# Input combinations by transposes and shared passes, first weights split a product ahead, bias tables read from one reversed row, log1p as a series

## The chip, the cores and the metric

One core of a Trainium2 chip runs the whole program. It has five engines with instruction queues of their own: TensorE (PE, matrix products; PEld is its loading of weights), VectorE (DVE), ScalarE (ACT), GpSimd (POOL) and SyncE (SP), and 16 DMA engines that move data between HBM and the core's memories SBUF and PSUM. DMAs are issued from a queue of an engine, here nearly all from SP and some from POOL and ACT. The metric is the device time of one execution in microseconds, as the median of several.

## The reference

One layer of an encoder runs on two inputs with shared weights: a sequence of 1024 rows ("A") and one of 512 rows ("B"), each row 1024 wide. Cut to what matters:

```python
h = rms_norm(x, pre_w)
cols = h @ w_in                     # q|k, v, o, z, gates of the mLSTM; q, k, v, z of the attention; merge gates
qk = silu(centred_dwconv(m_qk))     # short convolution along the rows
li = m_i + i_bias;  lf = log_sigmoid(m_f + f_bias)
y_m = mlstm(q, k, v, li, lf, both directions) * sigmoid(o) * silu(z)
# attention: 3 dilation groups x 8 heads x 64, each with a band of keys
logits = q @ k.T + bias_table[bucket(key - query)]
y_a = denominator_weighted_mix(softmax parts of the 3 groups) * silu(a_z)
merged = sig(g_A) * (y_m @ w_pm) + sig(g_B) * (y_a @ w_pa)
y = x + rms_norm(merged @ w_out, post_w)
```

Everything is float32. The products are made from a high and a low part of each operand (hi = rounded copy, lo = rest): three passes of PE, hi*hi, hi*lo and lo*hi (mm3, L206 to L211).

## The kernel before, in words

The 1024 rows of A and the 1024 columns of D are each cut in two halves of 512, so the input is a 2x2 matrix of blocks (a0, b0 for the first 512 rows, a1, b1 for the others). The input projection of A multiplies these with 2x2 blocks of weights by a scheme of seven block products in place of eight, which needs sums of the input's blocks (the seven names B11, T2, B21, T3, T1, T4, B22) and sums of the weights' blocks. Each of the seven combinations of the input is kept turned (features on partitions, rows along the free side) as a hi part H[0] and a lo part H[1] of four chunks of 128x512.

combos (L371 to L441) makes them, in group 0 of the values. lead and norm scale the rows; sub forms differences of blocks on DVE in place. put(m, k) makes one chunk of combination m in one PSUM bank. For T1 and T2 it turns four 128x128 blocks by transposes (L428). For B21 and B22 it turns them by float32 matmuls with the identity as the moving operand (L430). T3 and T4 have two terms: the first is turned by a transpose, the second added by a float32 matmul with plus or minus the identity (L430 again). A float32 matmul or a transpose of 128x128 shows as two records each or as one. Then ACT copies the bank to the hi part (L432); the lo part is DVE's difference (L434), or for B21 and B22 a pass of PE that subtracts the hi part in the bank (L438, with minus the identity as weights) and a second ACT copy (L439). The names in the profile: x is a block, d a PSUM bank, Hh and Hl the hi and lo parts, minus lies in a part of Hl.

value_group (L454 to L662) makes one of four groups of 322 value columns: products m1 (of B11), m2 (B21), m6 (T2), m7 (T3), m5 (T1), m4 (T4), m3 (B22), each of 48 passes of 128x322 in four banks. Weights arrive as va and vb (two halves of 644 KB each; SP issues them, L466 and L468, and each has one buffer); sums (L444 to L449) makes their sums with three DVE operations of 128x1288; split (L472 to L480) makes hi on ACT and lo on DVE. In group 0 the puts of the combinations are put between the passes of the products m1, m2, m7 and m6: with_m1 makes B21, with_m2 makes B22 and the first chunks of T3, and so on. u2 and u3 are running sums in SBUF; out writes a result part out by ACT (L509), DVE (L510) and an SP store (L511). The scheduler keeps each engine's program in the order in which the code issues the work, except that split runs with high priority, and issue_after pins an instruction behind another.

Then the unit pairs follow (unit_pair, L704): for each pair of 128 columns the same seven products of 128x512, weights loaded by SP (pw_raw, L682), summed on POOL (psum_w) and split by ACT and DVE (phla and phlb, L668 and L669). After the pairs the results are convolved or activated, and stored by SP (aqk_a, L219).

bias_tables (L342) makes, on 32 rows, for each of four cases of dilation and eight heads the bias by offset: a row of 512 numbers (erow, 2 KB in HBM). bias_copies (L360) copies two rows 128 times each to erep (512 KB), called once after a pair for 16 pairs, on SP behind that pair's weight loads. In the attention, table (L1322) loads for two heads the band of 128 partitions by a diagonal read of erep (a step of 511 from partition to partition), and DVE adds it to the logits (L1374).

lanes (L929) makes the logarithms of the gates on 64x128 tiles: log_sigmoid(x) = min(x, 0) - log1p(exp(-|x|)). log1p is made from Ln and Exp on ACT, with a correction, in L948 to L954. Such functions need another function table, whose loading shows as ACT_TABLE_LOAD. For B the generator lanes is advanced at chosen steps of the attention of A.

Of the kernel before, what the change touches and what calls it, by code (L numbers as in the profile page):

```python
# [29 lines left out]
P = 128  # L30
# [10 lines left out]
EL = 512  # L41
OW = 132
# [139 lines left out]
class Net:  # L182
# [23 lines left out]
    def mm3(self, out, lhs, rhs, start, stop):  # L206
        nc = self.nc
        (lh, ll), (rh, rl) = lhs, rhs
        nc.tensor.matmul(out, lh, rh, start=start, stop=False)  # L209
        nc.tensor.matmul(out, lh, rl, start=False, stop=False)  # L210
        nc.tensor.matmul(out, ll, rh, start=False, stop=stop)  # L211
# [127 lines left out]
    def bias_tables(self, sb, ps, dram):  # L339
# [18 lines left out]
        self.erep = dram.tile([m, 8, P, EL], F32, name="erep")  # L358

    def bias_copies(self, j, after):  # L360

        i, h = divmod(2 * j, 8)
        with self.tc.issue_after(after.ins):
            self.nc.sync.dma_start(self.erep[i, h:h + 2],
                                   self.erow[8 * i + h:8 * i + h + 2][:, None, :].to_broadcast([2, P, EL]))
# [6 lines left out]
    def combos(self, ps, H, xt, r, junk, pw, minus, again, diag):  # L372
# [45 lines left out]

        def put(m, k):
# [3 lines left out]
            p = ps.tile([P, BLK], F32, name="d")  # L423
            for t in range(4):
                for i, (x, one) in enumerate(terms[m]):
                    of, to = x[t][:, k * P:(k + 1) * P], p[:, t * P:(t + 1) * P]
                    if i == 0 and m not in (B21, B22):
                        nc.tensor.transpose(to, of, one)  # L428
                    else:
                        nc.tensor.matmul(to, of, one, start=t == i == 0, stop=True, skip_group_check=True)  # L430
# [13 lines left out]
    def sums(self, wa, wb, s):  # L444
# [4 lines left out]
        nc.vector.tensor_sub(s[:, 1], s[:, 0], wa[:, 0])  # L449
# [4 lines left out]
    def value_group(self, g, T, H, sb, us, co, ps, late=None, begin=None, u3=None, more=None, turn=None):  # L454
# [8 lines left out]
        if g:  # L463
            first, wa, wb, s = place(), *self.value_weights(sb)
            for kh in range(2):
                nc.sync.dma_start(wa[:, kh], self.a["w_vp"][g, 0, kh])  # L466
            for kh in range(2):
                nc.sync.dma_start(wb[:, kh], self.a["w_vp"][g, 1, kh])  # L468
        else:
            first, wa, wb, s, (lead, norm, sub, put) = begin  # L470

# [10 lines left out]
        def product(m, w, turns=(), outer=False):  # L482

            banks = [ps.tile([P, BLK], F32, name="d") for _ in range(4)]
# [3 lines left out]
            for i in range(4):  # L488
                for j in range(4):
# [3 lines left out]
                             k == 0, k == 3)  # L493
# [27 lines left out]
        if g == 0:  # L521
# [44 lines left out]
            def with_m7():  # L566
# [6 lines left out]
                put(T2, 0), put(T2, 1)  # L573
                yield
                put(T2, 2), put(T2, 3)
# [24 lines left out]
            with self.tc.issue_after(low[1]):  # L600
                s2 = split(s[:, 1])
# [8 lines left out]
        else:  # L610
            self.sums(wa, wb, s)
# [1446 lines left out]
```

## Time and profile before

| | |
|---|---|
| median of 3 runs | 2242.16 us (2238.9 to 2243.58) |
| the profiled execution, its own time | 2237.88 us |
| its span | 2236.1 us |
| PE busy | 2222.0 us, 99% of the span, clock granted 1.0 throughout |
| DVE, ACT, POOL busy | 1517.3, 1125.7 and 706.6 us |

The profiled execution's time is 1.8 us longer than its span, the part around the first and the last instruction. A row of a group gives busy time and the mean of one instruction; since matmuls overlap in PE's pipeline, the time from the start of one to the start of the next is what one costs, not its own duration. In the timeline the brackets at the end of a row tell how long the engine stood idle ahead of it, and what ended that.

### The profile page before, as it was taken

To read this page: it belongs to the slowest core of one execution; us is meant where nothing else is said; L and a number is where in the kernel's file an instruction comes from. 1 tells how busy PE (TensorE), PEld (TensorE's weight loads), DVE (VectorE), ACT (ScalarE), POOL (GpSimd) and SP (SyncE) were. 2 spreads that over 40 slices of the span, in tenths; PEclk is the share of its full clock that TensorE was granted. 3 is DMA by queue.
4 is the path that set the end of the run, shared out by engine and by line. 5 is a ranking of instruction groups with operands and counts; after the bars stand their busy time and mean duration, and the time that the engine had idled before them with its cause. 6 is when DMAs were issued, how large, how long until landed. Compare 5 with 4: busy or idle time off the path is not lost.

```text
span 2236.1 us, 35149 instructions
## 1 busy us (share of the span) xinstructions
PE 2222.0 (99%) x12050; PEld 1945.2 (87%) x12050; DVE 1517.3 (68%) x2975; ACT 1125.7 (50%) x2397; POOL 706.6 (32%) x976
## 2 busy tenths in 40 slices
PE   9999999999999999999999999999999999999998
PEld 8999878888888888888888889999888888888887
DVE  7765577677777655548887765565689855655774
ACT  6332244444444343447776665666665644554332
POOL 1000333343333222236677620011165522221221
PEclk9999999999999999999999999999999999999999
DMA  3552445543333222375755769997678888776663
GB/s 124 154 150 74 175 180 211 197 172 126 109 109 113 85 85 91 124 273 195 233 168 181 202 176 248 258 262 230 203 242 293 253 263 233 236 261 195 238 229 110
DMA packets 221788, 417.21 MB, mean 187 GB/s; under 512 B 24969, under 2 KB 128073, under 8 KB 221610
## 3 DMA queue, kind: packets, MB, share of 16 engines
q1 hardware_dynamic: 193640, 314.81, 44.2%
q0 software_dynamic: 24368, 87.56, 12.6%
q10 hardware_dynamic: 3602, 12.59, 1.4%
q8 instruction: 96, 1.57, 0.3%
q14 instruction: 82, 0.67, 0.1%
HBM read 295.14 MB, written 128.12 MB: 189 GB/s over the span
## 4 chain that ended last, share of the span: by engine, by line
PE 93%; DMA 3%; DVE 1%; issue 1%; ACT 1%; POOL 0%; DVEq 0%; POOLq 0%; SPq 0%; ACTq 0%
PE d L211 13%; PE d L210 13%; PE d L209 13%; PE dense L209 12%; PE dense L211 12%; PE dense L210 12%; PE o L1406 3%; PE pt L1385 2%; PE lg L1360 2%; PE num L209 1%; PE num L211 1%; PE num L210 1%; DMA vs_a<-vz 1%; PE a L1076 1%; PE kv L209 1%
## 5 line engine op out<-in xcount | busy, mean ns | idle before, releaser
L209 PE MATMUL dense<-H,wh 128*128 128x512 f32 x664 | 270.2, 407 | 0.0
L211 PE MATMUL dense<-H,wl 128*128 128x512 f32 x664 | 260.6, 393 | 0.0
L210 PE MATMUL dense<-H,wh 128*128 128x512 f32 x664 | 260.5, 392 | 0.0
L211 PE MATMUL d<-Hh,phla 128*128 128x512 f32 x608 | 236.8, 389 | 0.5 <-DVE phla L669 0.5
L209 PE MATMUL d<-Hh,phla 128*128 128x512 f32 x608 | 236.6, 389 | 0.5 <-ACT phla L668 0.5
L210 PE MATMUL d<-Hl,phla 128*128 128x512 f32 x608 | 236.5, 389 | 0.0
L278 DVE TENSOR_TENSOR wl<-wraw,wh 128x1024 fp32r<-128x1024 f32 (+1 forms) x121 | 149.2, 1234 | 66.0 <-ACT wh L272 65.7
L1374 DVE CUSTOM_DVE_ANT_0 ls<-lg,bias 128x256 f32<-128x256 f32 (+2 forms) x336 | 103.1, 333 | 117.8 <-PE lg L1360 53.5
L211 PE MATMUL d<-Hh,phlb 128*128 128x512 f32 x456 | 177.4, 389 | 0.0
L209 PE MATMUL d<-Hh,phlb 128*128 128x512 f32 x456 | 177.4, 389 | 0.0
L210 PE MATMUL d<-Hl,phlb 128*128 128x512 f32 x456 | 177.4, 389 | 0.0
L687 POOL TENSOR_TENSOR psum_w<-pw_raw 128x512 f32<-128x512 f32 x38 | 59.5, 1565 | 367.1 <-DMA pw_raw<-w_in 205.6
L1378 ACT ACTIVATE ls<-ls,nm 128x128 f32<-128x128 f32 (+1 forms) x288 | 125.3, 437 | 93.8 <-DVE nm L1376 61.4
L272 ACT ACTIVATE wh<-wraw 128x1024 fp32r<-128x1024 f32 (+1 forms) x124 | 128.7, 1038 | 70.7 <-PE dense L210 27.1
L211 PEld LDWEIGHTS dense<-H,wl 128*128 128x128 f32 x664 | 124.7, 188 | 27.9
L209 PE MATMUL d<-vhi,Hh 128*128 128x322 f32 x448 | 140.9, 314 | 0.3
L211 PE MATMUL d<-vhi,Hl 128*128 128x322 f32 x448 | 140.2, 313 | 0.4 <-DVE Hl L396 0.2
L210 PE MATMUL d<-vlo,Hh 128*128 128x322 f32 x448 | 139.7, 312 | 0.1
L210 PEld LDWEIGHTS dense<-H,wh 128*128 128x128 f32 x664 | 125.3, 189 | 14.3
L209 PEld LDWEIGHTS dense<-H,wh 128*128 128x128 f32 x664 | 125.1, 188 | 14.5
L211 PEld LDWEIGHTS d<-Hh,phla 128*128 128x128 f32 x608 | 114.1, 188 | 24.8 <-DVE phla L669 1.2
L209 PEld LDWEIGHTS d<-Hh,phla 128*128 128x128 f32 x608 | 114.1, 188 | 24.5 <-ACT phla L668 1.0
(572 smaller groups left out, 6116.3 us busy)
## 6 DMA issues: line engine op xcount, KB each, us to landing
pw_raw<-w_in SPq DMA_DIRECT2D x76, 512.0 KB
wraw<-w_in SPq DMA_DIRECT2D x64, 512.0 KB
aqk_a<-pwk SPq DMA_DIRECT2D x48, 512.0 KB
aqk_b<-sw SPq DMA_DIRECT2D x48, 256.0 KB
wraw<-w_pm POOLq DMA_DIRECT2D x24, 512.0 KB, 6.1
wraw<-w_out POOLq DMA_DIRECT2D x24, 512.0 KB, 3.9
wraw<-w_v POOLq DMA_DIRECT2D x22, 430.0 KB, 6.8
erep<-erow SPq DMA_DIRECT2D x16, 512.0 KB
```

The lines of the kernel that those rows point to most:

```text
L209: nc.tensor.matmul(out, lh, rh, start=start, stop=False)
L210: nc.tensor.matmul(out, lh, rl, start=False, stop=False)
L211: nc.tensor.matmul(out, ll, rh, start=False, stop=stop)
L272: high = nc.scalar.activation(hi[:, :n], raw[:, :n], AF.Copy)
L278: low = (self.lows or nc.vector).tensor_sub(lo[:, :n], raw[:, :n], hi[:, :n].bitcast(F32))
L687: self.nc.gpsimd.tensor_add(s[:, 0], ws[1][:, 0], ws[1][:, 1])
L1076: nc.tensor.matmul(p[:, c - c0], kT[:, ct, c * P:(c + 1) * P], qT[:, ct, c * P:(c + 1) * P], start=ct == 0, stop=ct == 1)
L1360: nc.tensor.matmul(lg[:, hh], q[hh][:, qs], z.rearrange("p (n j) -> p n j", j=P)[:, pair], start=z is k[hh], stop=z is not k[hh])
L1374: nc.vector.tensor_tensor_reduce(out=ls[rows, hh], in0=ts["lg"][hh][rows, of], in1=bt[rows, hh, by], scale=1.0, scalar=NEG, op0=OP.add, op ...
L1378: self.held = self.held[-3:] + [nc.scalar.activation(ls[:, hh], ls[:, hh], AF.Exp, bias=nm[:, hh:hh + 1], accum_out=ot[:, 128 + hh:129 + hh])]
L1385: nc.tensor.transpose(pp[:, hh * nk + x], ts["ls"][:, hh, x * P:(x + 1) * P], self.ident)
L1406: nc.tensor.matmul(po[:, hh * 64:hh * 64 + 64], pt[:, hh * nk + x], vh(kt[x], hh), start=x == 0, stop=x == nk - 1)
```

## The change

- put turns B21, B22 and T3's first term by transposes only. T3 is now a1 turned minus the split B22, made by two 128x512 passes (hi and lo part of B22, minus the identity as weights); its sign is turned, so u3 = u2 - m7 here and in the unit pairs. T4 is made from the split B21 and T2 by four such passes, without a transpose, with a plus identity made by one ACT copy. B22 takes over the bank of B21. One put of T2 moves a chunk earlier.
- In group 0, m2 is added on the banks of m1 by PE, and the sum is copied out by ACT instead of added by DVE. The last sum of weights moves behind the start of m7, the split for m7 and the difference T1 move ahead of m2.
- For groups 1 to 3 the loads of va and vb are issued by POOL and the first split of the next group is placed behind m4 (opening); the split for m3 stands ahead of that, the sums behind the split; out of m4 stands behind the split.
- The bias rows are stored reversed; erep and its 16 copies go; table reads erow itself, one element further per partition, and DVE reads the table backwards.
- log1p is a series on DVE in e/(2+e) (with a reciprocal), without Ln and the second Exp on ACT. For B lanes has one more stop, and is advanced at every 8th step instead of every 10th.

```diff
 EL = 512
+LOG1P = [1.0 / ((2 * k + 1) * 4 ** k) for k in range(1, 9)]
...
-    return m.reshape(-1, EL)
+    return m.reshape(-1, EL)[:, ::-1]
...
-        self.erep = dram.tile([m, 8, P, EL], F32, name="erep")
-
-    def bias_copies(self, j, after):
-
-        i, h = divmod(2 * j, 8)
-        with self.tc.issue_after(after.ins):
-            self.nc.sync.dma_start(self.erep[i, h:h + 2],
-                                   self.erow[8 * i + h:8 * i + h + 2][:, None, :].to_broadcast([2, P, EL]))
...
-        plus, neg = self.ident, minus.bitcast(F32)
-        terms = {B21: [(b0, plus)], B22: [(b1, plus)], T3: [(b1, plus), (a1, neg)],
-                 T1: [(a0, plus)], T2: [(b1, plus)], T4: [(b0, plus), (b1, neg)]}
+        turned = {B21: b0, B22: b1, T3: a1, T1: a0, T2: b1}
+        others = {T3: [(B22, minus)], T4: [(B21, plus), (T2, minus)]}
         def lead():
             ps_ = [ps.tile([P, BLK], F32, name="d") for _ in range(4)]
...
                 else:
                     nc.vector.tensor_sub(b1[t], b1[t], a0[t])
+        banks = {}
+
         def put(m, k):
             if m == T4 and k == 0:
                 again()
-            p = ps.tile([P, BLK], F32, name="d")
-            for t in range(4):
-                for i, (x, one) in enumerate(terms[m]):
-                    of, to = x[t][:, k * P:(k + 1) * P], p[:, t * P:(t + 1) * P]
-                    if i == 0 and m not in (B21, B22):
-                        nc.tensor.transpose(to, of, one)
-                    else:
-                        nc.tensor.matmul(to, of, one, start=t == i == 0, stop=True, skip_group_check=True)
+            p = banks.pop((B21, k)) if m == B22 else ps.tile([P, BLK], F32, name="d")
+            banks[m, k] = p
+            begun = m in turned
+            for t in range(4) if begun else ():
+                nc.tensor.matmul(p[:, t * P:(t + 1) * P], turned[m][t][:, k * P:(k + 1) * P], self.ident, is_transpose=True,
+                                 start=t == 0, stop=True, skip_group_check=True)
+            for of, one in others.get(m, ()):
+                for x in range(2):
+                    nc.tensor.matmul(p, one, H[x][of][:, k], start=not begun, stop=True, skip_group_check=True)
+                    begun = True
             hi, lo = H[0][m][:, k], H[1][m][:, k]
             nc.scalar.activation(hi, p, AF.Copy)
             if m not in (B21, B22):
...
-        nc.vector.tensor_sub(s[:, 1], s[:, 0], wa[:, 0])
+        return lambda: nc.vector.tensor_sub(s[:, 1], s[:, 0], wa[:, 0])
...
-        if g:
-            first, wa, wb, s = place(), *self.value_weights(sb)
-            for kh in range(2):
-                nc.sync.dma_start(wa[:, kh], self.a["w_vp"][g, 0, kh])
-            for kh in range(2):
-                nc.sync.dma_start(wb[:, kh], self.a["w_vp"][g, 1, kh])
-        else:
-            first, wa, wb, s, (lead, norm, sub, put) = begin
-
...
+        def opening(g):
+            wa, wb = (sb.tile([P, 2, N], F32, name=x, bufs=1) for x in ("va", "vb"))
+            for j, w in enumerate((wa, wb)):
+                for kh in range(2):
+                    nc.gpsimd.dma_start(w[:, kh], self.a["w_vp"][g, j, kh])
+            return wa, wb, split(wa[:, 0]), self.splits[1]
+
+        if g:
+            wa, wb, w11, early = self.opened
+            s = sb.tile([P, 2, N], F32, name="vsum", bufs=1)
+        else:
+            first, wa, wb, s, (lead, norm, sub, put) = begin
+
+        def product(m, w, turns=(), outer=False, onto=None):
+
+            banks = onto or [ps.tile([P, BLK], F32, name="d") for _ in range(4)]
             turns = iter(turns)
             if outer:
                 next(turns)
...
                     self.mm3(banks[t][:, :VW], (H[0][m][:, k, ts], H[1][m][:, k, ts]), (w[0][:, k], w[1][:, k]),
-                             k == 0, k == 3)
+                             k == 0 and onto is None, k == 3, skip_group_check=onto is not None)
...
-                put(T2, 0), put(T2, 1)
+                put(T2, 0), put(T2, 1), put(T2, 2)
                 yield
-                put(T2, 2), put(T2, 3)
+                put(T2, 3)
...
-                self.sums(wa, wb, s)
-            m2 = product(B21, w12, with_m2())
+                last = self.sums(wa, wb, s)
+            w7 = split(wb[:, 0])
+            with self.tc.issue_after(low[0]):
+                sub(T1)
+            m2 = product(B21, w12, with_m2(), onto=m1)
             held = []
             for t in range(4):
                 held.append(tile_("u2b", 4))
-                add(held[t], u2[t], m2[t][:, :VW])
-            with self.tc.issue_after(low[0]):
-                sub(T1)
-            m7 = product(T3, split(wb[:, 0]), with_m7())
+                nc.scalar.activation(held[t], m2[t][:, :VW], AF.Copy)
+            m7 = product(T3, w7, with_m7())
+            with self.tc.issue_after(low[1]):
+                last()
+                s2 = split(s[:, 1])
             for t in range(4):
-                add(u3[t], u2[t], m7[t][:, :VW])
-            with self.tc.issue_after(low[1]):
-                s2 = split(s[:, 1])
+                nc.vector.tensor_sub(u3[t], u2[t], m7[t][:, :VW])
...
-            self.sums(wa, wb, s)
-            m1 = product(B11, split(wa[:, 0], first))
+            with self.tc.issue_after(early.ins):
+                self.sums(wa, wb, s)()
+            m1 = product(B11, w11)
...
         m4 = product(T4, split(wb[:, 1]))
+        if g < 3:
+            w3 = split(s[:, 1])
+            self.opened = opening(g + 1)
         for t in range(4):
             add(u3[t], u3[t], m4[t][:, :VW])
-            out(t, 0, 1, u3[t])
+            with self.tc.issue_after(self.splits[0].ins):
+                out(t, 0, 1, u3[t])
         yield
-        m3 = product(B22, split(s[:, 1]))
+        m3 = product(B22, w3 if g < 3 else split(s[:, 1]))
...
-        nc.vector.tensor_add(u3, u2, m7)
+        nc.vector.tensor_sub(u3, u2, m7)
...
-        nc.vector.tensor_scalar(u1, e, 1.0, None, op0=OP.add)
-        nc.scalar.activation(l, u1, AF.Ln)
-        nc.vector.scalar_tensor_tensor(u1, u1, 1.0, e, op0=OP.subtract, op1=OP.subtract)
-        nc.scalar.activation(e, l, AF.Exp, scale=-1.0)
-        nc.vector.tensor_mul(e, e, u1)
-        nc.vector.tensor_sub(l, l, e)
+        nc.vector.tensor_scalar(u1, e, 2.0, None, op0=OP.add)
+        nc.vector.reciprocal(l, u1)
+        nc.vector.scalar_tensor_tensor(e, e, 2.0, l, op0=OP.mult, op1=OP.mult)
+        nc.vector.tensor_mul(u1, e, e)
+        nc.vector.tensor_scalar(l, u1, LOG1P[-1], None, op0=OP.mult)
+        for x in LOG1P[-2::-1]:
+            nc.vector.scalar_tensor_tensor(l, l, x, u1, op0=OP.add, op1=OP.mult)
+        nc.vector.scalar_tensor_tensor(l, l, 1.0, e, op0=OP.add, op1=OP.mult)
+        if apart:
+            yield
...
-            e = self.erep[CASES.index((g, dil)), 2 * pr:2 * pr + 2]
+            j = 8 * CASES.index((g, dil)) + 2 * pr
             for hh in range(2):
-                eh = e[hh]
+                e = self.erow[j + hh]
                 self.queue(("table", u), None, b[:, hh],
-                           bass.AP(tensor=eh.tensor, offset=eh.offset + 255 + c, ap=[[EL - 1, P], [1, W]]))
-            return b
+                           bass.AP(tensor=e.tensor, offset=e.offset + 257 - c - W, ap=[[1, P], [1, W]]))
+            return b[:, :, ::-1]
...
-                        if 0 < rows <= 16:
-                            N.bias_copies(rows - 1, q)
-                        rows += 1
...
-                    lanes = N.lanes(B, N.pool(s3, "lane2", 1, "right"), lambda: N.bank("o").rearrange("p a b -> p (a b)"))
+                    lanes = N.lanes(B, N.pool(s3, "lane2", 1, "right"), lambda: N.bank("o").rearrange("p a b -> p (a b)"), True)
                     N.attend(A, fill, STEPS[1], kept["qkv"], ("pt", "o", "lg"), 10, hold("head", lambda: N.ml_load(B, 0)),
-                             lanes, range(44, 96, 10))
+                             lanes, range(44, 96, 8))
```

More of the change, by code (lines that the diff above doesn't have):

```diff
@@ L927, in gate_tile, with lanes @@
         self.nc.sync.dma_start(T.gb, self.a[f"gb{T.n}"])
-    def lanes(self, T, sb, bank):
+    def lanes(self, T, sb, bank, apart=False):
         nc, n = self.nc, T.n
@@ L1790, in body @@
                 xt = [[xp[i].tile([P, D], F32, name=f"x{i}{t}") for t in range(4)] for i in range(2)]
-                minus = H[1][T4][:, 3, :P]
+                minus, plus = (H[1][T4][:, 3, i * P:(i + 1) * P] for i in range(2))
                 spare = H[0][T4].bitcast(F32).rearrange("p a c -> p (a c)")
@@ L1810, in body @@
                 nc.scalar.activation(minus, N.ident, AF.Copy, scale=-1.0)
+                nc.scalar.activation(plus, N.ident, AF.Copy)
                 opened = []
@@ L1869, in body @@
                     w = lambda dt=F32: wk.tile([P, 2 * BLK], F32R, name="pwk").bitcast(dt)
-                    rows = 0
                     for kind, i in ([("att", j) for j in range(0, 24, 2)]
```

18 lines of the change are left out of this document (8 added, 10 removed).

## The prediction

> **What bounds the kernel now.** I read the page's busy table and its chain first, then a table of windows by stage, then the waits of TensorE, and only then single stretches of the timeline.
>
> ```profile
> span 2236.1 us, 35149 instructions
> PE 2222.0 (99%) x12050; PEld 1945.2 (87%) x12050; DVE 1517.3 (68%) x2975; ACT 1125.7 (50%) x2397; POOL 706.6 (32%) x976
> ...
> PE 93%; DMA 3%; DVE 1%; issue 1%; ACT 1%; POOL 0%; DVEq 0%; POOLq 0%; SPq 0%; ACTq 0%
> ```
>
> TensorE (PE) is busy for 2222.0 of 2236.1 us, so only 14.1 us of waiting exist in the whole kernel. An edit can gain in two ways only: fewer PE passes, or a piece of those 14.1 us. It loses by every new wait on PE. The windows (columns: window, length, then busy time and count of PE, PEld, DVE, ACT and POOL, granted clock, DMA share, GB/s) tell where the idle time lies.
>
> ```profile
> 13.60:75.00 61.40, 60.40 (x442) 58.68 (x443) 51.60 (x79) 32.78 (x60) 3.70 (x5) 1.00 0.23 81
> 75.00:190.00 115.00, 114.94 (x767) 114.10 (x766) 82.27 (x153) 42.20 (x75) 0.34 (x2) 1.00 0.57 152
> ...
> 303.00:330.00 27.00, 25.93 (x113) 20.80 (x113) 21.01 (x22) 12.13 (x13) 7.39 (x5) 1.00 0.47 178
> 330.00:860.00 530.00, 530.00 (x2340) 438.87 (x2339) 379.04 (x390) 222.59 (x222) 179.81 (x145) 1.00 0.36 133
> ...
> 1320.00:1700.00 380.00, 379.26 (x2459) 355.26 (x2458) 241.31 (x844) 249.65 (x768) 73.86 (x128) 1.00 0.88 250
> ```
>
> The first window holds the input combinations, the second value groups 1 and 2, the third the start of the unit pairs, the fourth the rest of them, the last the first attention. PE is full in all. In the first one DVE is busy for 51.6 of 61.4 us, so DVE and ACT can become the bound there once PE gets shorter. Of the waits of PE (total, times, longest) one bears on the lanes' edit; the others that matter stand in the timelines below:
>
> ```profile
> PE o L1406 <- DVE pts L1390: 0.7, 1, 0.7
> ```
>
> **Input combinations.** These rows are the PE timeline of that stretch (start, us, instruction); a put is one 128x512 chunk of a combination.
>
> ```profile
> 19.51 1.05 PE L430 MATMUL d<-ident,x 128*128 128x128 f32 x8
> 20.32 0.39 PE L209 MATMUL d<-vhi,Hh 128*128 128x322 f32 x1
> ...
> 26.51 0.31 PE L209 MATMUL d<-vhi,Hh 128*128 128x322 f32 x1
> ...
> 28.29 1.95 PE L430 MATMUL d<-ident,x 128*128 128x128 f32 x16
> 29.99 0.39 PE L209 MATMUL d<-vhi,Hh 128*128 128x322 f32 x1
> ...
> 33.57 0.71 PE L438 MATMUL d<-Hh,Hl 128*128 128x512 f32 x2
> 34.12 0.31 PE L209 MATMUL d<-vhi,Hh 128*128 128x322 f32 x1
> ...
> 43.38 0.39 PE L209 MATMUL d<-vhi,Hh 128*128 128x322 f32 x1
> ...
> 50.61 1.04 PE L428 MATMUL d<-ident,x 128*128 128x128 f32 x8
> 51.40 0.39 PE L209 MATMUL d<-vhi,Hh 128*128 128x322 f32 x1
> ...
> 66.26 0.27 PE L428 MATMUL d<-ident,x 128*128 128x128 f32 x1
> ...
> 67.51 0.39 PE L209 MATMUL d<-vhi,Hh 128*128 128x322 f32 x1
> ```
>
> Prices from start to next start: a put by matmuls against the identity (L430, eight records for four blocks) takes 20.32 - 19.51 = 0.81 us; two of them 29.99 - 28.29 = 1.70 us. Two puts by transposes (L428, eight records for eight blocks) take 51.40 - 50.61 = 0.79 us, 0.40 each. A put of two terms, transposes and matmuls in turn, takes 67.51 - 66.26 = 1.25 us. Two 128x512 passes take 34.12 - 33.57 = 0.55 us, 0.275 each; in the long pair stage it is 530.00/2340 = 0.226 us each.
>
> B21, four puts: matmuls become transposes, 0.81 to 0.40, at most -1.6 us on PE. What then ends last is ACT, which alone makes both halves of each chunk:
>
> ```profile
> 24.40 0.60 ACT L432 ACTIVATE Hh<-d 128x512 fp32r<-128x512 f32 x1
> 24.89 0.59 ACT L439 ACTIVATE Hl<-d 128x512 fp32r<-128x512 f32 x1
> ```
>
> Hi copy, PE's subtraction and lo copy pass from hand to hand, about 1.1 us for a chunk, while PE's own step was 0.81 + 0.33 us. So I count half, -0.8 us; the bounds are 0 and -1.6.
>
> B22, four puts under product m2: ACT has 7 us for them and PE sets the time: 4 x (0.85 - 0.40) = -1.8, taken as -1.7 us. T3, four puts: four transposes and two passes against the split B22, 0.40 + 0.55 = 0.95 for 1.25 to 1.29, -0.3 each, -1.3 us in all. T4, four puts: four passes and no transpose, between 4 x 0.226 = 0.90 and 4 x 0.275 = 1.10 for 1.25; I take 0.95 as they run back to back, -0.3 each, -1.2 us. T3 now needs both halves of B22; they come some 2 us ahead of it, as now for the product. The put of T2 moved a chunk earlier does the same work. Product m2 accumulates on the banks of m1: four DVE adds become four ACT copies, beside PE. It must now wait until ACT has copied m1 out, which is behind it at 22.84 us, before m2's start at 26.51:
>
> ```profile
> 21.42 1.42 ACT L586 ACTIVATE u<-d 128x322 f32<-128x322 f32 x4
> ```
>
> One sum of weights (1.5 us on DVE) moves into the stretch between m7 and m6, where m6's first chunk waits for DVE now; that costs 0 to 0.6 us there, which I leave to the range.
>
> Sum of the combinations: -0.8 - 1.7 - 1.3 - 1.2 = -5.0 us, between -3.0 (B21 nothing, T4 at 1.10 each, m6 0.6 later) and -6.2 us (all by PE's count).
>
> **Bias tables.** The copies of the reversed rows into a spread-out table (L364, 16 stores of 512 KB on SP) go; the 48 pairs of table loads read one row at 128 offsets instead. In the pair stage one such copy stands ahead of four stores, and a wait follows:
>
> ```profile
> 305.86 0.60 SPq L364 DMA_DIRECT2D erep<-erow  x1
> 307.71 5.41 SPq L219 DMA_DIRECT2D aqk_a<-pwk  x4
> ```
>
> ```profile
> 320.80 0.66 ACT L776 ACTIVATE pwk<-c 128x256 fp32r<-128x256 f32 x1 [9.67 <-DMA aqk_a<-pwk]
> ```
>
> ```profile
> 321.54 0.39 PE L211 MATMUL d<-Hh,phla 128*128 128x512 f32 x1
> 322.46 0.50 PE L209 MATMUL d<-Hh,phla 128*128 128x512 f32 x1 [0.54 <-ACT phla L668]
> 322.79 0.40 PE L210 MATMUL d<-Hl,phla 128*128 128x512 f32 x1
> 323.72 0.50 PE L211 MATMUL d<-Hh,phla 128*128 128x512 f32 x1 [0.53 <-DVE phla L669]
> ```
>
> ACT stands 9.67 us for a store issued 13 us before; the weights split behind it on ACT (phla) come late, and PE waits twice. Starts stand 322.46 - 321.54 = 0.92, 0.33 and 323.72 - 322.79 = 0.93 us apart where a pass takes 0.23: 0.69 + 0.10 + 0.70, about 1.4 us. Without the copy's 512 KB in the queues the store should land earlier, and 1.4 us are the bound, since PE can't be more than full; the other bound is 0, where the store is slow by itself. I take -1.4, because this copy is what SP issues right ahead of the late stores. All later pair work shows no wait, so the other 15 copies give nothing. The reads of one row: the only wait of DVE for a table now is the last row here, and DMA is at 0.88 there, so I price the loads at nothing with 0 to 2.7 us as the range. DVE (L1374) reads the table backwards; the nearest rows are the lanes' copies, half of which run forwards and half reversed (L1004: lowest, median and highest ns):
>
> ```profile
> L1374 DVE CUSTOM_DVE_ANT_0 ls<-lg,bias x336: 275/292/467, 1317.5 to 2070.2; 128x128 f32<-128x128 f32 x64, 128x256 f32<-128x256 f32 x56, 64x128 f32<-64x128 f32 x48
> ...
>   DMA bias<-erep: 2.7, 1
> ```
>
> ```profile
> L1004 DVE COPY l_q<-l_li x4: 191/211/218, 157.6 to 1469.5; 32x128 f32<-32x128 f32 x4
> ```
>
> They lie within 13%, so a backward step costs nothing in them: 0. The Trainium skill, "Vector Engine (DVE) Microarchitecture Reference", section 5.1, lists how the engine streams an operand with a negative step as not measured, so it neither supports nor denies this reading.
>
> **The value groups.** The weights of groups 1 to 3 are loaded by POOL instead of SP, and the first split of the next group is put behind m4 instead of m3. PE shows no wait there now (114.94 of 115.00 us), so nothing is gained. What can be lost is in these rows, the loads of group 2 as issued now, the first use of the second pair, the last copy out of m1, and a load on POOL's queue:
>
> ```profile
> 122.07 0.82 SPq L468 DMA_DIRECT2D vb<-w_vp  x2
> ```
>
> ```profile
> 129.68 1.50 DVE L447 TENSOR_TENSOR vsum<-vb 128x1288 f32<-128x1288 f32 x1
> ```
>
> ```profile
> 148.48 0.42 ACT L614 ACTIVATE u<-d 128x322 f32<-128x322 f32 x1
> ```
>
> ```profile
> wraw<-w_v POOLq DMA_DIRECT2D x22, 430.0 KB, 6.8
> ```
>
> vb is issued when its split is done (122.07), on whichever queue. POOL has nothing long ahead of it there (0.34 us busy in the window). On POOL's queue 430 KB land in 6.8 us, so 644 KB in about 10.2 us by bytes. If the two halves run beside each other they land at 132 and the sums follow with slack: DVE has until m2 of that group, at about 147, where the last part of m1 ends and ACT is about to copy it (148.48). Cost 0.
>
> **The lanes' log1p.** ACT loses two pairs of small activations and four table loads (the two at one of these lines are below, lowest, median and highest ns); DVE gains some nine operations per call, at 0.28 us (the second row) 2.5 us, twice. Both run beside PE.
>
> ```profile
> L949 ACT ACT_TABLE_LOAD  x2: 1283/1283/1283, 113.6 to 1462.3; - x2
> ```
>
> ```profile
> 115.96 0.28 DVE L950 SCALAR_TENSOR_TENSOR l_u<-l_u,l_e 64x128 f32<-64x128 f32 x1
> ```
>
> The second call lies near the 0.7 us wait of L1406, so it may cost or give 0.7 us; I take 0.
>
> **Sum.** -5.0 - 1.4 = -6.4 us: span 2236.1 to 2229.7, profiled execution 2237.9 to 2231.5. The profiled run is 4.3 us below the median of 2242.16, so against the median 2242.2 - 6.4 = 2235.8 us, 0.3% faster. About 0.2%, 4.5 us, is what a measurement of this kernel can tell from no change.
>
> **Rivals.**
> 1. Part of the gain goes: ACT and DVE bound the first window (51.6 of 61.4 us busy, a chunk of B21 at 1.1 us on ACT), or the pair stage's store stays late. Then the gain is between 3.0 and 5.0, say 4.0 us: 2238.2 us, mostly within 0.2%.
> 2. It is more: the loads, freed of 16 stores of 512 KB, or the shorter ACT chain also remove the 0.7 us wait of L1406 and m6's first wait; 8.5 us, 2233.7.
> 3. Slower: POOL's loads come late. If the halves of va and vb follow one another at 10.2 us each, vb is whole at 122.1 + 20.4 = 142.5 and not before 129.7; DVE stands at the first sum, and behind it in its queue lie m3's adds, two more sums (3.0 us) and the split for m2 (1.5 us), some 8.5 us: 151 for 147, 4 us at each of three boundaries, +12 - 6.4 = +5.6, 2247.8 us. It decides where a second half lands over 16 us after its issue. Against it: 6.8 us for 430 KB while other loads run. A rule of the Trainium skill speaks for it: "SBUF — State Buffer", "SBUF: two separate sides", says that a DMA issued by POOL cannot have its descriptors written while DVE runs an operation in a two-port mode, and that DMAs issued by SP or ACT run beside DVE. No run here shows that wait so far.
> 4. Slower: the backward read runs at half rate. L1374 is 336 operations of 292 ns, so up to 98 us more on DVE; in the attention DVE has 139 us free (380 - 241), so most is hidden, and where 15% shows (14 us) the time is 2242.2 + 14 - 6.4 = 2249.8. It decides above about 3% shown. The rows of L1004 speak against it.
>
> **How the numbers follow.** Forecast 0.47 (own range 2234 to 2238); rival 1 0.24 (0.06 of it faster, the rest within 0.2%); rival 2 0.10; rival 3 0.12; rival 4 0.07. Faster: 0.47 + 0.06 + 0.10 = 0.63, less 0.01 for a forecast that just misses the bound: 0.62; within: 0.18 and that 0.01; slower 0.19. The range 2230 to 2246 takes in all but most of rivals 3 and 4.
>
> **What would show it.** In the changed profile: m2 of group 0 starts near 25.7 instead of 26.5, m7 near 39.7 instead of 43.4, m5 near 62.5 instead of 67.5; L1374's median stays at 0.29 us; the window from 303 to 330 loses its two waits; PE's busy time falls by about 5 us and its idle time by 1.4. Wrong if PE shows waits at the starts of groups 1 to 3 (sums, splits), if the first window ends under 3 us earlier, or if the attention grows.

## The result and the profile after

The changed kernel takes 2234.57 us as the median of 19 runs (2232.1 to 2239.49), the kernel before 2241.95 us in the same rounds (2237.32 to 2245.27): a ratio of 0.9971, with a 95% interval of 0.9965 to 0.9978, or 7.4 us less. 2235.8 us and "faster" had been forecast. The profiled execution of the changed kernel lies above its median (2236.86 us) and that of the kernel before below its own (2237.88 us), so the two spans differ by 1.0 us only; what the parts are worth must be read inside them.

The page of the changed kernel, its busy row:

```profile
span 2235.1 us, 34988 instructions
...
PE 2218.1 (99%) x11962; PEld 1939.6 (87%) x11962; DVE 1523.7 (68%) x2989; ACT 1120.3 (50%) x2394; POOL 715.7 (32%) x988
```

Its windows (columns as before: window, length, busy time and count of PE, PEld, DVE, ACT and POOL, granted clock, DMA share, GB/s):

```profile
13.60:75.00 61.40, 59.99 (x395) 56.67 (x394) 53.67 (x82) 36.92 (x69) 5.98 (x9) 1.00 0.40 118
75.00:190.00 115.00, 115.00 (x763) 113.35 (x762) 83.02 (x158) 37.61 (x69) 4.62 (x10) 1.00 0.52 136
...
303.00:330.00 27.00, 27.00 (x120) 22.35 (x120) 19.04 (x22) 10.38 (x11) 7.72 (x5) 1.00 0.31 117
...
1320.00:1700.00 380.00, 376.55 (x2424) 352.38 (x2423) 239.43 (x837) 241.62 (x752) 73.47 (x127) 0.99 0.88 245
```

PE has 3.9 us less to do (2218.1 for 2222.0), although some passes run slower here, as below. Its idle time, forecast to fall by 1.4 us, rose from 14.1 to 17.0 us (2235.1 - 2218.1). The value groups show no wait on PE (115.00 of 115.00), and the pair stage's two waits are gone (27.00 of 27.00). The attention got worse, 376.55 of 380 us busy for 379.26, and its clock fell below 1.00; that the attention grows is one of the signs that the prediction named for being wrong.

A better measure than a window is the lead: the start of each PE instruction in one profile, minus the start of the same one in the first profile of the kernel before (both timelines laid side by side; minus is earlier). The columns are places, in us of the profile of before; the rows are the profiles of this study, one execution each. The place 14.5 lies ahead of the first combination, and there even two executions of one kernel differ (-0.30 and -1.14 for the changed one), so what a part is worth is read as a difference between two columns:

```
            14.5   26.6   43.4   67.6    303    360    900   1440   1520   2200
changed    -0.30  -1.16  -4.51  -6.12  -6.57  -8.37  -8.37  -6.50  -0.26  -0.52
again      -1.14  -2.00  -5.38  -7.02  -7.47  -9.27  -9.26  -9.07  -3.77  -0.75
spread     -1.35  -2.22  -5.59  -7.23  -6.97  -6.79  -6.79  -6.35  -0.62  -1.14
oldlog     -0.32  -1.18  -4.61  -6.25  -6.70  -8.50  -8.49  -7.41  -3.13  -2.80
spload     -1.05  -1.91  -5.26  -6.90  -7.35  -9.15  -9.15  -8.22  -5.86  -6.31
before2    +0.12  +0.11  +0.11  +0.13  +0.04  -0.61  -0.61  -0.35  +1.03  +0.83
core       -0.42  -1.28  -4.61  -6.22  -6.64  -4.11  -4.10  -3.56  -0.06  -0.66
mm         -0.16  -0.14  -1.77  -3.41  -3.86  -5.66  -5.66  -4.74  -2.44  +0.30
plain      -0.25  -1.11  -4.54  -6.18  -6.63  -8.43  -8.43  -8.33  -2.28  -2.68
halfafter  -0.66  -1.52  -4.95  -6.59  -7.04  -8.85  -8.84  -7.75  -7.99  -7.93
halfbefore +0.00  +0.01  +0.01  +0.02  +0.88  +0.43  +0.43  +2.40  +3.39  +4.04
late       -0.59  -1.45  -4.82  -6.40  -6.85  -8.65  -8.65  -8.19  -3.07  -1.19
fillsp     -0.79  -1.64  -5.07  -6.68  -7.13  -8.93  -8.92  -1.51  +2.65  +3.41
```

By 360 us the changed kernel is 8.4 us ahead. It is still 8.4 us ahead at 900, 6.5 at 1440, and 0.3 us are left of it at 1520. That last loss has these rows on PE:

```profile
1493.57 1.19 PE L1397 MATMUL pt<-ident,ls 128*128 128x128 f32 x4 [2.07 <-ACT ls L1390]
1494.40 0.71 PE L211 MATMUL dense<-X,H 128*128 128x430 f32 x1
1494.91 0.56 PE L212 MATMUL dense<-X,H 128*128 128x430 f32 x1
1495.26 0.56 PE L213 MATMUL dense<-X,H 128*128 128x430 f32 x1
```

and this one on ACT:

```profile
1490.79 0.92 ACT L274 ACTIVATE wh<-wraw 128x860 fp32r<-128x860 f32 x1 [5.25 <-DMA wraw<-w_v]
```

and this window:

```profile
1490.00:1504.00 14.00, 11.85 (x62) 10.92 (x62) 6.58 (x32) 7.46 (x26) 2.19 (x3) 0.76 1.05 278
```

ACT stands 5.25 us for a weight load of the fill (the other work between the attention's passes). The exponentials of the attention (L1390) are behind it in ACT's queue, and PE waits 2.07 us for them. After that PE's passes of 430 columns start 0.35 us apart instead of 0.20, for some 6 us: the trace gives half the clock for 6.8 us. The Trainium skill, "TensorE: Matmul & The Clock Gate", Part 1, says that the clock is halved after a window of 3.4 us with PE idle and judged in such windows. The length agrees (stretches of 3.41 and 6.83 us were seen in these profiles), the condition does not: PE waited 2.07 us here in all, not 3.4, and less than 1.4 us of that had passed when the clock fell (1.00 from 1492.0 to 1492.7, 0.50 from 1492.9 on, with the wait beginning at 1491.50).

### The profile page after: what moved, and what is told of

It reads as the page before. It is cut to its first block, busy times and chain, and to the rows that moved or that the text cites. A ratio compares the mean times of both kernels' runs of the same rounds, so it can differ in the third digit from the quotient of the medians.

```text
span 2235.1 us, 34988 instructions
## 1 busy us (share of the span) xinstructions
PE 2218.1 (99%) x11962; PEld 1939.6 (87%) x11962; DVE 1523.7 (68%) x2989; ACT 1120.3 (50%) x2394; POOL 715.7 (32%) x988
## 4 chain that ended last, share of the span: by engine, by line
PE 94%; issue 2%; DMA 2%; DVE 1%; ACT 1%; POOL 0%; SPq 0%; DVEq 0%; POOLq 0%; ACTq 0%
PE d L213 14%; PE d L211 14%; PE d L212 14%; PE dense L211 12%; PE dense L213 12%; PE dense L212 12%; PE o L1418 3%; PE pt L1397 2%; PE lg L1372 2%; PE num L213 1%; PE num L211 1%; PE num L212 1%; PE a L1088 1%; PE kv L211 1%; PE kv L212 1%
## 5 line engine op out<-in xcount | busy, mean ns | idle before, releaser
L1390 ACT ACTIVATE ls<-ls,nm 128x128 f32<-128x128 f32 (+1 forms) x288 | 124.8, 435 | 92.7 <-DVE nm L1388 58.9
```

What stands on the lines that cost most here:

```text
L1390: self.held = self.held[-3:] + [nc.scalar.activation(ls[:, hh], ls[:, hh], AF.Exp, bias=nm[:, hh:hh + 1], accum_out=ot[:, 128 + hh:129 + hh])]
```

## The experiments

**again.** The changed kernel as it is, no edit.

> The changed kernel once more, unchanged. In its first profile PE stood 8.4 us earlier than before at the end of the unit pairs, and 0.5 us earlier at the end; 5.1 us of that went at 1485 to 1500 us, a wait of 2.07 us for a late weight load of the fill and 6.8 us at half the granted clock behind it. Theory: that wait is a matter of one execution, since the median gained 7.4 us; then this profile has a span near 2230 us and no such wait, and the time is 7 us below that of before (ratio 0.997). Rival: the wait belongs to the changed order of loads in the attention; then it stands here too, within 0.5 us, with a span near 2235.

2237.09 us (2234.41 to 2240.95, 11 runs) against 2241.92, 0.9981 with 0.9973 to 0.9990, in other rounds than the first comparison, so 4.8 us less instead of 7.4. The wait near 1490 is there again, 0.41 and 1.06 us, with two more at 1463 and 1464 for loads of keys, and again a stretch at half the clock:

```profile
1462.86 0.35 PE L1372 MATMUL lg<-V0a,Q 128*128 128x256 f32 x1 [0.86 <-DMA V0a<-aqk_a]
1464.04 0.36 PE L1372 MATMUL lg<-V0b,Q 128*128 128x256 f32 x1 [0.83 <-DMA V0b<-aqk_a]
1491.13 0.38 PE L1372 MATMUL lg<-V1b,Q 128*128 128x256 f32 x1 [0.41 <-DMA V1b<-aqk_a]
1492.57 0.93 PE L1397 MATMUL pt<-ident,ls 128*128 128x128 f32 x4 [1.06 <-ACT ls L1390]
```

The theory is out and the rival holds as far as that the loss comes back (span 2234.9 us): it is no accident of one execution. That the order of the loads makes it is not shown by this. 5.3 us of the lead go between 1440 and 1520, and 3.0 more behind 1520; mm and late lose 2.7 and 1.9 there too. Among these are single waits of PE of 1.19 us at 1851.89 (again), 1.23 at 1853.55 (mm) and 1.17 at 1728.99 (late), whose cause was not tried.

**spread.** The spread-out bias tables come back.

```diff
-    return m.reshape(-1, EL)[:, ::-1]
+    return m.reshape(-1, EL)
+        self.erep = dram.tile([m, 8, P, EL], F32, name="erep")
+    def bias_copies(self, j, after):        # as before, called for 16 pairs
...
-                e = self.erow[j + hh]
+                eh = e[hh]                  # e is erep of this case and pair
-            return b[:, :, ::-1]
+            return b
```

> Only the spread-out bias tables come back: 16 copies of 512 KB on SP in the pair stage, forward diagonal reads. Theory: the store behind the first copies is late again, ACT stands for it, and PE waits twice in the second pair; PE's lead over the kernel before falls from 8.4 to about 6.7 us at 360 us of the span, and the time is 1.7 us above the changed kernel's. Rival 1: the lead at 360 us stays at 8.4, the wait was one of the value groups' loads. Rival 2: the loads from one row are what is late in the attention (5.8 us of DVE waits for them against 2.7 before); then this kernel loses the 1.7 us but gains 2 to 5 us there, and is faster than the changed one.

2237.14 us, 0.9984 (0.9975 to 0.9993). The lead falls from 7.63 us at 150 to 6.79 at 360, where again's grows from 7.42 to 9.27. The waits of PE between 290 and 330 us are back (total, times, longest):

```profile
PE d L213 <- DVE phla L685: 1.1, 2, 0.5
PE d L211 <- ACT phla L684: 0.7, 1, 0.7
```

The changed kernel has none there. So in these two profiles removing the copies is worth 2.7 us up to 360 us, against a kernel that has the combinations too, in two pairs and not in one. The whole time does not show it: 1.7 us above the changed kernel were expected, and the medians of spread and again, taken in the same rounds, are 0.05 us apart, with intervals of about 2 us on either side. The loss at 1440 to 1520 is as large with the old tables (5.7 us), so reading one row isn't its cause. Reading backwards costs nothing either; the row of the changed kernel for that operation has the same median, 292 ns, as before:

```profile
L1386 DVE CUSTOM_DVE_ANT_0 ls<-lg,bias x336: 220/292/425, 1311.3 to 2069.4; 128x128 f32<-128x128 f32 x64, 128x256 f32<-128x256 f32 x56, 64x128 f32<-64x128 f32 x48
```

**oldlog.** Ln and Exp with their tables, the old stops.

```diff
-        nc.vector.tensor_scalar(u1, e, 2.0, None, op0=OP.add)
-        nc.vector.reciprocal(l, u1)
...
+        nc.vector.tensor_scalar(u1, e, 1.0, None, op0=OP.add)
+        nc.scalar.activation(l, u1, AF.Ln)
...
-                             lanes, range(44, 96, 8))
+                             lanes, range(44, 96, 10))
```

> Only the logarithm comes back as Ln and Exp with its table loads, with the stops of the lanes as before. Theory: all of it is beside PE, the time is that of the changed kernel within 1 us, and PE's lead at the end of the pairs is 8.4 us as there. Rival: the longer run of small DVE operations (a reciprocal of 0.95 us and ten more) at 1455 to 1466 us is what delays the attention there; then PE has no wait of 2 us at 1485 to 1500 here and the time is 3 to 5 us lower.

2234.61 us, 0.9971 (0.9959 to 0.9982), 6 runs. Between again and this stand 2.5 us, but the intervals overlap, and the waits at 1440 to 1520 are as many, only not in the same places: 1.22 us of them is PE at 1464.60 waiting for DVE behind two reloads of ACT's tables (1.28 us each, at 1456.38 and 1458.85), the wait of L1406 in before. The stretch costs 4.3 us here.

**spload.** The weights of value groups 1 to 3 come by SP.

```diff
-                    nc.gpsimd.dma_start(w[:, kh], self.a["w_vp"][g, j, kh])
+                    nc.sync.dma_start(w[:, kh], self.a["w_vp"][g, j, kh])
```

> Only the weights of value groups 1 to 3 are loaded by SP again, at the same places. Theory: PE never waits for them on either queue, the lead over the kernel before at 300 us is 6.6 us in both, and the time is the same within 1 us. Rival: the loads on POOL leave SP free for the stores (the wait of the second pair hangs on SP); then the lead at 360 us falls by 1 to 2 us.

2235.35 us, 0.9974 (0.9965 to 0.9983). From 150 to 360 us the lead runs as in the changed kernel (1.85 us more in both), so the queue of these loads is worth nothing and takes nothing there. A wait of 0.78 us near 960 (for a one-element memset of DVE, L795) is in the changed kernel and in eight other profiles with the change, and not in this one, nor in mm and the three of the old order. The queue is not its cause, since core and plain load by SP as well and have it; its cause stays open.

**before2.** The kernel before, once more.

> The kernel before, a second execution with a profile. Four profiles of kernels with the change lose 2.4 to 6.6 us between 1440 and 1520 us of the span, each with a wait of 0.8 to 2.1 us of PE near 1492; the first profile of before lost nothing there, but it is one of the fastest of its runs (2237.9 for a median of 2241.9). Theory: before has that wait too in most executions; then this one shows waits near 1496 of 0.5 us or more and a span near 2240. Rival: only the change brings it; then none is here, and a slower time of before comes from elsewhere.

One run, 2238.72 us. Its waits near there are 1.23 us at 1470.80 and 0.20 at 1497.39, its loss from 1440 to 1520, against the first profile, is 1.4 us, and no clock is lost. The theory holds in part: the kernel before loses something there too, less than those with the change. But both of its profiles are of executions below the median (2237.88 of 2241.95 us, 2238.72 of 2240.81), so what its longer ones lose there no profile shows.

**core.** Combinations and openings alone; the edits of spread, oldlog and spload together.

> The input combinations and the opening of the value groups alone: spread-out bias tables, old logarithm and stops, weights of the groups on SP are back. Theory: 5.8 us from the combinations (0.9 for B21, 3.4 for B22 and T3, 1.5 for T4) and 0.4 in the groups, the pair stage's wait stays; lead 6.2 us at 360 us plus what the first loads give (0.3 to 1.3), time 6 us below before. Rival, from my prediction: the combinations give 5.0.

2237.22 us, 0.9983 (0.9974 to 0.9992), 3.6 us below before by the medians where 6 were expected. The combinations are worth what was expected: -0.42 at 14.5 to -6.22 at 67.6, 5.8 us. But at 360 the lead is 4.1 us. In the same pair as in before, the store now holds ACT for 10.63 us and PE for 1.50, and after these waits PE is slower, starts 0.42 apart for 0.23:

```profile
315.13 0.65 ACT L792 ACTIVATE pwk<-c 128x256 fp32r<-128x256 f32 x1 [10.63 <-DMA aqk_a<-pwk]
```

```profile
316.78 0.50 PE L211 MATMUL d<-Hh,phla 128*128 128x512 f32 x1 [1.50 <-ACT phla L684]
...
318.04 0.50 PE L213 MATMUL d<-Hh,phla 128*128 128x512 f32 x1 [0.53 <-DVE phla L685]
...
319.60 0.63 PE L212 MATMUL d<-Hl,phla 128*128 128x512 f32 x1
320.02 0.63 PE L213 MATMUL d<-Hh,phla 128*128 128x512 f32 x1
```

Half the clock for 3.41 us by the trace. In this profile the combinations without the bias rows give back 2.5 us of their gain at the first copies.

**mm.** B21 and B22 by matmuls again.

```diff
-... self.ident, is_transpose=True,
+... self.ident, is_transpose=m not in (B21, B22),
```

> The changed kernel with B21 and B22 turned by matmuls with the identity again, all else as changed. The prediction's steps: B21's transposes give 0.8 us up to the start of m2 (ACT sets the time), B22's give 1.7 us from there to m7; so m2 starts 0.8 us later and the lead at 68 us is 2.5 us smaller than the changed kernel's. Rival: a record is what costs, and ACT bounds B21 whole; then m2 starts at the same time and 1.7 us are lost.

One run, 2237.68 us. m2 starts at 26.36, with ACT's wait as in before, for 25.36 in the changed kernel; from 14.5 on this is 0.02 - (-0.86), 0.9 us for B21. B22's part, from there to m7, is 3.35 - 1.63 = 1.7 us. Both as predicted (0.8 and 1.7).

```profile
26.03 0.50 PE L435 MATMUL d<-Hh,Hl 128*128 128x512 f32 x1 [0.46 <-ACT Hh L429]
26.36 0.32 PE L211 MATMUL d<-vhi,Hh 128*128 128x322 f32 x1
...
28.15 1.95 PE L422 MATMUL d<-ident,x 128*128 128x128 f32 x16
29.85 0.39 PE L211 MATMUL d<-vhi,Hh 128*128 128x322 f32 x1
```

**plain.** The old logarithm and SP's loads together, all else as changed (the edits of oldlog and spload).

> The changed kernel with the old logarithm and its stops and with the groups' weights on SP: the parts kept are the combinations, the openings and the bias rows. Theory: the runs of small DVE operations and the extra stop delay the attention near 1465 us, and the kernel is 1 to 3 us below the changed one, with a granted clock above 0.999. Rival: these parts cost nothing and the changed kernel's losses there are chance; then the time is the same within 1 us.

2234.84 us, 0.9978 (0.9969 to 0.9986): the changed kernel's time within the intervals, and its loss (6 us from 1440 to 1520, with half the clock for 3.4 us). Neither of these parts is the cause. Core differs from this kernel in the bias rows alone and was timed in the same rounds: its median is 2.4 us above, at the edge of what these numbers of runs can tell.

**halfafter and halfbefore.** The fill's weight loads in the attention of A are cut to half their bytes, in the changed kernel and in the one before.

```diff
-        self.loaded = self.side.dma_start(raw[:, :kt * cols], src)
+        n = kt * cols // (2 if self.side is self.nc.gpsimd and getattr(self, "half", 0) else 1)
+        self.loaded = self.side.dma_start(raw[:, :n], src[:, :n])
```

> The changed kernel with the fill's weight loads of the attention of A cut to half their bytes (the second halves of these value weights are stale, so outputs of the fill are not computed rightly); 2.2 to 4.5 MB of some 47 MB between 1310 and 1495 us are gone. Six profiles with the change lose 2.4 to 6.6 us between 1440 and 1520 us, where the DMA share is about 1.0. Theory: those waits are loads that come late in that saturated stretch; then PE has no wait over 0.3 us at 1460 to 1500 here, no lower clock behind it, and keeps its lead: 1520 us stands at -6 to -8 us against the first profile of before. Rival: the lanes' small operations on DVE make the waits; then they stay, about 0.7 and 1 us, and the loss with them.

> The kernel before with the same loads of the attention of A cut to half (same outputs not computed rightly). Theory: before loses 1 to 3 us to late loads in most executions as well, so it gains that, 0.9985 to 0.9995 of before; and the difference of the two kernels with halved loads is the whole lead, 8 us (0.9963 between them), more than the 5 to 7 us between the two as they are. Rival: before loses nothing there; then the time is that of before within 0.5 us and the halved pair differs as the full pair does.

halfafter: 2230.83 us (2229.48 to 2233.43, 5 runs), 0.9955 (0.9942 to 0.9969). halfbefore: 2238.42 us (11 runs), 0.9988 (0.9979 to 0.9997). The only wait of PE in halfafter from 1440 to 1520, and the windows there, of halfafter, of the changed kernel and of the kernel before:

```profile
PE pt L1398 <- ACT ls L1391: 0.3, 1, 0.3
```

```profile
1440.00:1480.00 40.00, 40.00 (x277) 39.19 (x276) 28.64 (x125) 26.19 (x94) 2.73 (x5) 1.00 1.00 244
1480.00:1520.00 40.00, 39.67 (x273) 38.51 (x272) 23.04 (x100) 26.45 (x90) 10.27 (x13) 1.00 0.84 220
```

```profile
1440.00:1480.00 40.00, 38.70 (x264) 37.41 (x263) 27.53 (x120) 24.78 (x88) 2.19 (x4) 1.00 0.99 240
1480.00:1520.00 40.00, 37.84 (x241) 36.40 (x240) 20.27 (x90) 21.72 (x76) 7.98 (x11) 0.91 0.84 221
```

```profile
1440.00:1480.00 40.00, 39.26 (x270) 38.13 (x270) 24.60 (x108) 28.39 (x95) 2.19 (x4) 1.00 0.97 243
1480.00:1520.00 40.00, 40.00 (x279) 39.20 (x277) 25.36 (x110) 25.24 (x88) 8.28 (x11) 1.00 0.94 254
```

In halfafter, whose profile is of the lowest of its five executions, PE is full but for 0.33 us, the clock stays, and the lead is kept: -7.75 us at 1440, -7.99 at 1520, -7.93 at 2200. With the same new logarithm and stops the waits are gone once there are fewer bytes, so late loads make them. The DMA share is as high as ever from 1440 to 1480 (1.00 for 0.99, and 0.97 in before); what fell is ACT's longest wait for a load of the fill, from 5.25 to 2.6 us (1.7 in the first profile of before). The two halved kernels stand 7.6 us apart by their medians, 0.9955/0.9988 = 0.9967. Expected were 8. Within these rounds halving saves 3.2 us in the kernel before (2241.61 to 2238.42) and 4.3 us in the changed one, with late, below, standing for it (2235.17 to 2230.83). So by the times, unlike the profiles, late loads cost both kernels much the same, and the 1.1 us between the two are less than these runs can tell.

**late.** The lanes' stops moved out of that stretch.

```diff
-                             lanes, range(44, 96, 8))
+                             lanes, range(68, 96, 4))
```

> The changed kernel with the stops of the lanes of B at tiles 68 to 92 in steps of 4 instead of 44 to 92 in steps of 8, so that the logarithm's run of DVE operations leaves the stretch with DMA at 1.0 (1320 to 1500 us). Theory (loads are late, DVE is not the cause): the waits at 1460 to 1495 stay within 1 us and the time is the changed kernel's within 1 us, ratio 0.997 to 0.998. Rival: the lanes cause the waits; then they are gone, and the time is 2 to 4 us lower, ratio 0.9955 to 0.9965.

2235.17 us, 0.9973 (0.9963 to 0.9984), with waits at 1462 to 1492 of 0.26, 0.82, 1.01 and 1.25 us, and half the clock for 3.4 us behind them, while the series now runs at 1534 instead of 1456. The lanes don't cause them.

**fillsp.** The fill's loads by SP.

```diff
-                N.side = nc.gpsimd          # ahead of the attention of A
```

> The changed kernel with the fill's weight loads of the attention of A issued by SP instead of POOL, bytes unchanged. Theory: the 16 engines are full there and the queue makes no difference; the waits near 1490 stay between 0.8 and 2.1 us, ratio 0.997 to 0.998. Rival: POOL's queue is what makes those loads late; then the waits near 1490 go, and the ratio is that of the kernel with halved loads, near 0.9955, a version that beats both. Worse, 1.000, if loads on SP stand behind others that wait for buffers.

2243.13 us, 1.0010 (1.0000 to 1.0020), no better than the kernel before: the third case that was expected. POOL's queue is not what makes the loads late, and SP is worse. In the changed kernel POOL issues such a load 0.3 us after its buffer is free (1397.99 to 1398.29), SP here 6 and 10 us after (1396.22 to 1402.57, 1402.21 to 1411.82), with other loads and stores between. ACT waits 5.75 us for one, PE 4.31, with half the clock for 6.8 us.

```profile
1418.00 0.92 ACT L274 ACTIVATE wh<-wraw 128x860 fp32r<-128x860 f32 x1 [5.75 <-DMA wraw<-w_v]
```

```profile
1419.46 0.91 PE L1418 MATMUL o<-K,pts 128*128 128x64 f32 x3 [4.31 <-ACT pts L1400]
```

No kernel that computes the whole output beats the changed one by more than the intervals.

## Why the prediction was right, point by point

The time, 2235.8 against 2234.57 us, is near partly by luck, from two errors of opposite sign: up to 360 us the first profile gains 8.1 us (from -0.30 to -8.37) where the sum had 6.4, and losses that the sum didn't have take 0.7 us of that by the first comparison (7.4) and 3.3 by the second (4.8).

B21: -0.8 predicted, -0.86 measured (from -0.30 to -1.16); ACT was indeed what ends last there, as the copies of the changed kernel still alternate without a gap from 22.39 to 25. B22 and T3: -3.0 predicted, -3.35 measured; mm gives 1.7 of that to B22, as predicted, so T3 and what else changed there give 1.6 for 1.3; a put of T3 takes 37.97 - 37.06 = 0.91 us, where 0.95 was priced. T4: -1.2 predicted. Its row in the changed kernel:

```profile
60.48 0.39 PE L426 MATMUL d<-Hh,Hl 128*128 128x512 f32 x1
60.71 0.39 PE L426 MATMUL d<-Hl,Hl 128*128 128x512 f32 x1
60.94 0.39 PE L426 MATMUL d<-Hh,Hl 128*128 128x512 f32 x1
61.16 0.39 PE L426 MATMUL d<-Hl,Hl 128*128 128x512 f32 x1
61.39 0.31 PE L211 MATMUL d<-vhi,Hh 128*128 128x322 f32 x1
```

Four passes take 61.39 - 60.48 = 0.91 us, the lower of my two bounds, and the four puts with m6's first chunk give 1.6 us. The combinations are worth 5.8 us, inside the range of 3.0 to 6.2; the turning of B21 and B22 in it was taken back by itself, the other parts were not.

The bias copies: -1.4 was predicted for one wait, and called a bound; its three terms, 0.69 + 0.10 + 0.70, add to 1.49. The wait was worth 1.8 us (from -6.57 to -8.37), and 2.7 in spread, where the earlier pairs bring a second one; between core and plain it is 4.4 (from 67.6 to 360), with half the clock in it. Against the two other profiles of the old order, before2 and halfbefore, it is 1.2 and 1.4 us, since PE waits once for 0.53 us there. The mechanism was the one named, a store behind the copy that holds ACT. But 1.4 us was no bound: one execution's waits were taken for the cost, and they change from one profile to the next.

The value groups: 0 predicted, 0.4 gained, from what was not tested. The rival of late loads on POOL did not happen. The halves of va and vb landed 4.4 to 11.4 us after their issue, where the rival needed over 16. And they have more time: vb is issued at 115.08 by POOL and first used at 129.13, 14 us for the 7.6 us of before (122.07 to 129.68), since its split now comes 7 us earlier:

```profile
115.08 1.07 POOL L474 DMA_DIRECT2D vb<-w_vp  x2 [17.11 <-DVE vlo L466]
```

```profile
129.13 1.49 DVE L444 TENSOR_TENSOR vsum<-vb 128x1288 f32<-128x1288 f32 x1
```

The lanes' logarithm: "beside PE" was not quite so. The old one held PE for 0.74 to 1.23 us near 1470 (before, before2, oldlog, core, plain, halfbefore); in halfafter, with fewer bytes to load, that wait is gone, in halfbefore it stays. It was one end of the 0.7 us that I named.

What the sum lacks is the attention: I let 6.4 us of gain pass through it unchanged. Kernels with the change that reach it 3.6 to 9.1 us earlier lose 2.3 to 6.2 us between 1440 and 1520 in single profiles (fillsp, halfafter apart), measured against the first profile of before, whose only wait there is 0.74 us; its second profile loses 1.4. Halving the fill's loads shows that late loads make the waits; that the clock then halves is in the records of six of them (changed, again, spread, plain, late, fillsp). Two things stay open. One is whether the changed kernels really lose more there than before: the profiles say so, but the medians (7.4 us in the first comparison, 4.8 in the second, 7.6 with halved loads) leave 0 to 3 us for it. The other is why they should: with all work shifted alike the loads should be late by the same amount, and DMA is about as full there in before (0.97 to 0.99 from 1320 to 1480 in both).

## What to carry to other kernels

Where PE is 99% busy, count its passes: transposing in one pass instead of matmuls against the identity, and building later combinations from already split ones, gave 5.8 us where 5.0 had been counted, from prices taken from start to start and not from durations. Look for what holds an in-order engine for a DMA; there 16 copies that nobody waited for cost 1.2 to 4.4 us in five profiles, through the store behind them. And before counting a gain through to the end, find the stretch after it in which DMA is full: here single profiles lost 2.3 to 6.2 us in it, and only fewer bytes took the waits away. A profile is one execution: set it beside the median before its loss is called the kernel's.

## What the runs showed of the hardware

Half the clock follows short waits. Stretches of 3.41 or 6.83 us at half clock came with waits of PE adding up to 1.1 to 2.1 us within about 3 us (2.07 in one in the changed kernel; 1.50 and 0.53 in core; 0.28 and 0.81 in plain; 1.25 in one in late), and 4.3 us in fillsp, while single waits of 1.22 to 1.35 us (oldlog, before2, halfbefore) were followed by none. So the length of the wait alone does not decide between 1.1 and 1.35 us, and what else does no run here shows. Each 3.41 us costs 1.7 us, so a wait of 2 us can cost 5. A reciprocal of 64x128 on DVE takes 0.94 us, over three times any of the other small operations of the series (0.21 to 0.29):

```profile
L957 DVE RECIPROCAL l_l<-l_u x2: 939/942/946, 108.1 to 1456.2; 64x128 f32<-64x128 f32 x2
```
